# Layer 1 of a hybrid RWKV-7 / attention / Hyena backbone: two scans run as one sequence

## The chip, the cores and the metric

The kernel runs on one core of a Trainium2 chip. That core has five engines with a program of their own each: TensorE (PE, with its weight loads as PEld), VectorE (DVE), ScalarE (ACT), GpSimd (POOL) and SyncE (SP), which issues most DMA transfers. Each engine takes its instructions in the order in which they were written down for it; semaphores order the engines among each other. The metric is the device time of one execution in microseconds, lower is better.

## The reference

Two layers work on 256 context tokens and 512 latent tokens of width 1024. Each layer normalises its tokens, projects them once, and hands the columns to three mixers (RWKV-7 in both directions, latent attention, Hyena convolution); a joint output projection and an expert network (PEER) follow. In the last layer only the latents go on, but the RWKV state that the latents start from and the attention keys and values of the context are still needed. Cut to the part that the change touches:

```python
def rwkv7_mixer(p_lat, p_ctx, ..., need_ctx):
    lr, lk, lv, ldec, la, lkk, lkr, lg = rwkv7_prepare(p_lat, *prm)
    cr, ck, cv, cdec, ca, ckk, ckr, cg = rwkv7_prepare(p_ctx, *prm)
    for d, rev in enumerate((False, True)):
        s_ctx, yc = rwkv7_scan(s0, cr, cdec[d], ckk, ca[d], ckr[d], cv, rev)
        _, yl = rwkv7_scan(s_ctx, lr, ldec[d], lkk, la[d], lkr[d], lv, rev)
    ...
    S = S * w_t - (S kk_t) (kk_t * a_t) + v_t k_t     # one step of a scan
    y_t = S r_t
# layer 1 (need_ctx is False): the context scan gives s_ctx and no y
    out = concat([rwkv, attention, hyena]) @ w_out    # waits for all three
```

## The kernel before

The six RWKV heads are three pairs (`j` = 0, 1, 2), one pair on 128 partitions. A scan is done in chunks of 64 tokens, both directions at once. A step of `rwkv` is one pair and one group of 256 tokens per direction (`s`): the context has one group a pair, the latents two, so layer 1 has three context steps and six latent steps. A step has two parts.

- `prep` (`rwkv_keys` for the first group of a pair, then `rwkv_group`) needs the projected columns but no state: decays by a scan along the tokens (`L`, `Pt`), the products `EH` and `FG`, and then the inverse of a triangular matrix by five levels of small products (`Ahz`, `X`, `Dz`, `Xz`), which go to and fro between PE, DVE and ACT. It ends with `Ktok` and `Btok`.
- `chain` (`rwkv_chain`) carries the state `S` through the four chunks of the group: `R`, `U`, then `S` (DVE, line 1052 is the last row of a chunk), for the latents also the output `Y`. After the second group of a latent pair, `rwkv_read` normalises `Y` and turns it back by 24 products on PE (lines 777 and 272, `rw<-ident,Y`, `rw<-eye,Y`).

In one call of `rwkv`, `merge` writes the `chain` of a step and the `prep` of the next one interleaved, so that the `prep` fills the waits of the `chain`. Layer 1 calls `rwkv` twice, first for the context and then for the latents. Between the calls it closes the pools of the context (`zc`, `rwk`, `rwp`) and opens `rwk` and `rwp` anew, at twice the width. The last `chain` of the context and the first `prep` of the latents therefore stand in different calls.

`layer1` weaves four tracks: `context_out`, `attention` (which projects latents and context, then runs `mla` for the context and for the latents), `scan`, and `hyenas`. `weave` always takes the track whose summed cost is lowest; the costs are the numbers that the generators yield, those of the scan times `RC1` = 0.05 for the context and `RL1` = 0.8 for the latents. What is woven is then put into its final order on each engine by the scheduler of the tile framework, which follows priority and readiness as it models them.

`mla` for the latents works on three groups of two heads. For a group it makes keys (`kTl`) and queries (`qT`) from `x`; then, for each head, eight products for the row maxima (`mm<-kTc,qT`, `mm<-kTl,qT`, reduced by DVE to `mx`, `top`), and six rounds of score product (`tr<-qT,...`), exponential on ACT (`PT`, line 1225) and product with the values (`mm<-PT,...`). The score tile `tr` has one buffer in PSUM, so that a round's score waits for the exponential of the round before. A reciprocal and a multiplication on DVE (lines 1231 and 1233) end a head. When scan, attention and Hyena are written, `mixed` begins the output projection (`mhi`, `mlo`, `mm<-mlo,wh`); it needs the heads of all three.

Of the kernel before, what the change touches and what calls it, by code (L numbers as in the profile page):

```python
# [10 lines left out]
F32 = mybir.dt.float32  # L11
# [11 lines left out]
TC, TL = 256, 512  # L23
# [127 lines left out]
RC1, RL1 = 0.05, 0.8  # L151
# [93 lines left out]
class K:  # L245
# [294 lines left out]
    def layer1(self):  # L540
        if self.done:
            return
        with ExitStack() as lay, ExitStack() as es:
            zl = self.open_layer(1, lay, 2)
            zkv = self.lp.tile([128, 2, TC], F32, name="zkv")
            yml = [zl[:, 11], zl[:, 15], zl[:, 12]]
            ctx = ExitStack()
            z = {}

            def scan():  # L550
                yield self.after("rwc")
                yield from self.scaled(self.rwkv(1, (0, z["c"], False)), RC1)
                ctx.close()
                self.rwk = [es.enter_context(self.pool(n, k)) for n, k in (("rwk", 1), ("rwp", 2))]
                self.mark("rw1")
                yield from self.scaled(self.rwkv(1, (1, zl, True)), RL1)

            def hyenas():
                yield from self.hyena_filters(1, 1, "left")
                self.mark("flt")  # L560
                yield self.after("rw1")
                yield from self.hyena(1, 1, zl, "left")

            def attention():
                self.wcut = 4
                yield from self.project(1, 1, [(m, zl[:, m]) for m in ORDER], "right", self.h1)
                self.wcut = 8
                self.scale_par()
                self.mark("pl1")
                yield self.after("xc1", "flt")  # L570
                self.open_rwkv(es)
                zc = z["c"] = ctx.enter_context(self.pool("zc")).tile([128, 7, TC], F32, name="zc")
                self.rwk = [ctx.enter_context(self.pool(n, k)) for n, k in (("rwk", 1), ("rwp", 2))]
                self.mark("rwc")
                yield from self.project(1, 0, [(m, zc[:, m - 3] if m < 10 else zkv[:, m - 19]) for m in ORDER if m in (3, 4, 5, 6, 7, 8, 9, 19, 20)], "right")
                yield from self.mla(1, 0, [None, None, zkv[:, 0], zkv[:, 1]], None, "right")
                yield from self.mla(1, 1, [zl[:, m] for m in range(17, 21)], yml, "right")

            self.weave((0, self.context_out()), (0, attention()), (0, scan()), (0, self.scaled(hyenas(), HL1)))
            es.close()  # L580
            self.open_late(1)
            self.flat(self.mixed(1, 1, [zl[:, 0], zl[:, 1], zl[:, 2], *yml, zl[:, 13], zl[:, 14]], "left"))
        if self.done:
            return
        self.flat(self.ffn(1))
        self.late.close()
        self.dump("xf11", [self.x[1][:, k] for k in range(8)])
# [188 lines left out]
        else:  # L776
            self.nc.tensor.transpose(out, src, self.ident[h, h])

    def rwkv(self, li, *jobs):

        nc = self.nc
        if self.done:
            return
        H = (slice(0, 64), slice(64, 128))
        wd, ws = self.rwd, self.rws
        wk, wp = self.rwk
        if True:
            W = max(TL if b else TC for b, _, _ in jobs)
            alloc = lambda n, T, **k: wk.tile([128, W], F32, name=n, **k)[:, :T]
            keys, vy, made = {}, {}, {}  # L790

            def parts(b, z, full, j):
                T = TL if b else TC
                o = 0 if full else -3
                return T, z[:, 9 + o], z[:, j] if full else None, z[:, 3 + o + j], z[:, 6 + o + j]

            def prep(b, z, full, j, s, ready):
                T, zd, zr, zk, zv = parts(b, z, full, j)
                nseg = T // 256
                if s == 0:  # L800
                    if j == 0:
                        yield self.after(*[("z", li, b, m) for m in ((9, 10) if full else (9,))])
                        nc.scalar.activation(zd[0:64], zd[0:64], AF.Tanh)
                        if full:
                            nc.scalar.activation(z[:, 10], z[:, 10], AF.Tanh, scale=0.5)
                            nc.vector.tensor_scalar(z[:, 10], z[:, 10], 0.5, 0.5, op0=OP.mult, op1=OP.add)
                    yield self.after(*[("z", li, b, m) for m in ((j, 3 + j, 6 + j) if full else (3 + j, 6 + j))])
                    keys[b, j] = self.rwkv_keys(j, T, zk, alloc)
                sg2 = (s, nseg - 1 - s)
                tok = [slice(256 * g, 256 * g + 256) for g in sg2]  # L810

                def dv(ap):
                    v = ap.rearrange("p (g t) -> p g t", t=256)
                    if nseg == 1:
                        return v[:, 0:1, :].to_broadcast([128, 2, 256])
                    return v if s == 0 else v[:, ::-1]

                made[b, j, s] = yield from self.rwkv_group(j, tok, dv, zd, zr, zk, *keys[b, j], full, wp, wd, ws, H, ready)

            def chain(b, z, full, j, s):  # L820
                T, zd, zr, zk, zv = parts(b, z, full, j)
                nseg, nch = T // 256, T // 64
                c3 = lambda ap: ap.rearrange("p (c t) -> p c t", t=64)
                if s == 0:
                    Vt = c3(alloc("Vt", T))
                    self.to_tok(Vt, [zv[:, 64 * c:64 * c + 64] for c in range(nch)])
                    vy[b, j] = Vt, c3(alloc("Y", T)) if full else None
                Vt, Y = vy[b, j]
                yield from self.rwkv_chain(j, s, (s, nseg - 1 - s), *made[b, j, s], Vt, Y, nch, full, ws, H)
                if s == nseg - 1:  # L830
                    if full:
                        self.rwkv_read(j, T, Y, zr, zk, Vt, z[:, 10], zr, alloc)
                        yield 5
                    if j == 2:
                        self.mark(("rwkv", li, b))

            steps = [(b, z, full, j, s) for b, z, full in jobs for j in range(3) for s in range((TL if b else TC) // 256)]
            yield from prep(*steps[0], self.after())
            for n, g in enumerate(steps):
                def scan(g=g, n=n):  # L840
                    yield from chain(*g)
                    self.mark(("chain", li, g[0], n))
                if n + 1 < len(steps):
                    yield from self.merge(scan(), prep(*steps[n + 1], self.after(("chain", li, g[0], n))))
                else:
                    yield from scan()

    def merge(self, *gens):

# [953 lines left out]
```

## Time and profile before

| What | Value |
|---|---|
| median of 3 runs | 5459.62 us (5457.41 to 5464.74) |
| profiled execution, own time | 5464.84 us |
| its span, first to last instruction | 5463.1 us |
| mean granted TensorE clock | 0.928 |
| busy share of PE, PEld, DVE, ACT, POOL | 90%, 69%, 70%, 35%, 23% |

The span is the time from the first to the last instruction of the profiled execution, and that execution took 1.7 us more than its span and 5.2 us more than the median. All times in the rows below are microseconds from the start of the span. The mixers of layer 1, where the change lies, stand between about 3380 and 4061 us.

### The profile page before, as it was taken

What the parts mean: (1) busy time and instruction counts of PE and PEld (TensorE: products, weight loads), DVE (VectorE), ACT (ScalarE), POOL (GpSimd) and SP (SyncE); (2) the same over time, 40 slices, a digit from 0 to 9 for tenths busy, and PEclk for the clock granted to TensorE, in tenths of its full rate; (3) what the DMA queues carried; (4) which work ended last, traced back from release to release, by engine and by line L of the source; (5) the groups of instructions that cost most, each with busy time, mean ns of one, the idle gap of its engine ahead of it and who ended that gap; (6) DMA issues with size and microseconds to landing.
All of it is one profiled execution on the core that took longest, in us unless ns stands there. A gap on an engine that the chain in (4) does not pass through costs nothing. (4 is left out here: it accounts for less than half of the span.)

```text
span 5463.1 us, 76042 instructions
## 1 busy us (share of the span) xinstructions
PE 4928.4 (90%) x28693; PEld 3745.5 (69%) x28693; DVE 3849.6 (70%) x8277; ACT 1918.5 (35%) x3438; POOL 1241.3 (23%) x933
## 2 busy tenths in 40 slices
PE   7987998889989999999999678888889889999998
PEld 4765676547644588887878456656657667888887
DVE  6356666656896488887888875656646985777776
ACT  5322222443254333333333232222223454444442
POOL 2322212221200122222222363211122321111110
PEclk9977899899999999999999889777899999999999
DMA  6300121342365788888888764200022668888885
GB/s 207 103 22 31 51 86 55 113 151 71 109 187 162 240 326 316 330 323 311 318 325 303 274 238 153 77 1 1 1 74 82 196 191 295 324 322 312 321 320 206
DMA packets 395517, 1028.18 MB, mean 188 GB/s; under 512 B 31780, under 2 KB 198981, under 8 KB 339597
## 3 DMA queue, kind: packets, MB, share of 16 engines
q1 hardware_dynamic: 339852, 620.65, 34.0%
q0 software_dynamic: 55296, 402.68, 19.6%
q8 instruction: 225, 3.69, 0.3%
q14 instruction: 144, 1.17, 0.1%
HBM read 920.19 MB, written 103.02 MB: 187 GB/s over the span
## 5 line engine op out<-in xcount | busy, mean ns | idle before, releaser
L203 POOL DMA_INDIRECT row<-in_uv,idx x384 | 531.8, 1385 | 1860.8 <-DVE acc L241 1586.7
L659 ACT ACTIVATE wh<-w 128x1024 fp32r<-128x1024 f32 (+1 forms) x557 | 571.0, 1027 | 1049.5 <-PE mm L272 461.7
L272 PE MATMUL mm<-hlo,wh 128*128 128x512 f32 (+2 forms) x2408 | 877.0, 368 | 30.7 <-DVE zl L688 7.5
L272 PE MATMUL mm<-hhi,wh 128*128 128x512 f32 (+2 forms) x2408 | 866.8, 364 | 0.0
L660 DVE TENSOR_TENSOR wl<-w,wh 128x1024 fp32r<-128x1024 f32 x424 | 516.3, 1221 | 255.0 <-ACT wh L659 252.1
L272 PE MATMUL mm<-hhi,wl 128*128 128x512 f32 (+2 forms) x2408 | 531.5, 361 | 1.7 <-POOL wl L660 1.7
L272 PEld LDWEIGHTS mm<-hlo,wh 128*128 128x128 f32 x2408 | 461.2, 192 | 104.4 <-issue 18.4
L241 DVE SCALAR_TENSOR_TENSOR acc<-row,act,acc 128x1024 f32<-128x1024 f32 x381 | 496.5, 1303 | 35.3 <-ACT act L237 34.6
L272 PEld LDWEIGHTS mm<-hhi,wh 128*128 128x128 f32 x2408 | 461.5, 192 | 61.8 <-issue 3.3
L219 DVE SCALAR_TENSOR_TENSOR row<-row,xk 128x1024 f32<-128x1024 f32 x384 | 480.3, 1251 | 16.5 <-DMA row<-in_uv,idx 16.3
L272 PE MATMUL mm<-row,wh 128*128 128x512 f32 (+1 forms) x1056 | 455.5, 574 | 29.9 <-DMA wh<-in_uT 25.1
L272 PEld LDWEIGHTS mm<-hhi,wl 128*128 128x128 f32 x2408 | 425.9, 189 | 56.6 <-issue 3.8
L660 POOL TENSOR_TENSOR wl<-w,wh 128x1024 fp32r<-128x1024 f32 (+1 forms) x133 | 291.4, 2198 | 670.0 <-ACT wh L659 405.3
L272 PEld LDWEIGHTS mm<-row,wh 128*128 128x128 f32 x1056 | 195.3, 195 | 211.2 <-issue 165.4
L236 ACT ACTIVATE act<-act 128x1 f32<-128x1 f32 x384 | 75.7, 197 | 498.6 <-DVE row L219 498.3
L1779 ACT ACTIVATE stage<-ch 128x512 f32<-128x512 f32 x224 | 218.2, 1101 | 62.6 <-PE ch L272 59.8
L1546 ACT ACTIVATE g<-mm 128x512 f32<-128x512 f32 (+1 forms) x256 | 137.6, 538 | 232.3 <-PE mm L272 197.2
L272 PE MATMUL rw<-wh,cl 128*128 128x512 f32 x512 | 201.5, 394 | 6.5 <-DVE cl L1614 3.5
L272 PE MATMUL rw<-wl,ch 128*128 128x512 f32 x512 | 200.5, 392 | 0.0
L272 PE MATMUL rw<-wh,ch 128*128 128x512 f32 x512 | 199.9, 390 | 0.0
L272 PE MATMUL ch<-wh,cl 128*128 128x512 f32 x512 | 199.6, 390 | 0.0
L272 PE MATMUL ch<-wh,ch 128*128 128x512 f32 x512 | 199.4, 389 | 0.0
(542 smaller groups left out, 10206.0 us busy)
## 6 DMA issues: line engine op xcount, KB each, us to landing
w<-in_uv SPq DMA_DIRECT2D x256, 512.0 KB
w<-in_uT SPq DMA_DIRECT2D x190, 512.0 KB
Wd<-stage SPq DMA_DIRECT2D x28, 2048.0 KB
w<-in_mod_w SPq DMA_DIRECT2D x192, 256.0 KB
wh<-in_uT SPq DMA_DIRECT2D x66, 512.0 KB
W<-Wd SPq DMA_DIRECT2D x32, 1024.0 KB
W<-Wd SPq DMA_DIRECT2D x32, 768.0 KB
w<-in_wq SPq DMA_DIRECT2D x32, 512.0 KB
```

The costliest lines, as they stand in the source:

```text
L203: self.nc.gpsimd.indirect_dma_start(out=row, out_offset=None, in_=self.k.io[f"uv{self.li}"], in_offset=bass.IndirectOffsetOnAxis(ap=self.t ...
L219: nc.vector.scalar_tensor_tensor(row[:, 0:1024], row[:, 0:1024], 1.0, self.x, op0=OP.mult, op1=OP.mult, accum_out=act)
L236: nc.scalar.activation(act, act, AF.Gelu)
L241: nc.vector.scalar_tensor_tensor(self.acc, row[:, 1024:], act, self.acc, op0=OP.mult, op1=OP.add)
L272: self.nc.tensor.matmul(out, lhsT, rhs, start=start, stop=stop, skip_group_check=True)
L659: self.nc.scalar.activation(wh[:, s], w, AF.Copy)
L660: eng.tensor_tensor(wl[:, s], w, wh[:, s].bitcast(F32), op=OP.subtract)
L1546: nc.scalar.activation(g, p[:, 0:ND], AF.Gelu)
L1779: nc.scalar.activation(stage[:, :, u:u + 4].rearrange("p a t -> p t a"), p, AF.Copy, scale=1 / GS)
```

## The change

Layer 1 now calls `rwkv` once with both jobs, so that `merge` also joins the last `chain` of the context with the first `prep` of the latents. The pools `rwk` and `rwp` are opened once, and `zc` stays open with them. The cost factor moves into `rwkv`: a merged step is scaled by the factor of the step whose `chain` it holds, so the first latent `prep` is now woven at `RC1` and no longer at `RL1`. The Hyena track waits for the mark that ends the context scan instead of the mark `rw1`.

```diff
-            ctx = ExitStack()
             z = {}
 
             def scan():
                 yield self.after("rwc")
-                yield from self.scaled(self.rwkv(1, (0, z["c"], False)), RC1)
-                ctx.close()
-                self.rwk = [es.enter_context(self.pool(n, k)) for n, k in (("rwk", 1), ("rwp", 2))]
-                self.mark("rw1")
-                yield from self.scaled(self.rwkv(1, (1, zl, True)), RL1)
+                yield from self.rwkv(1, (0, z["c"], False), (1, zl, True), cost=(RC1, RL1))
 
             def hyenas():
                 yield from self.hyena_filters(1, 1, "left")
                 self.mark("flt")
-                yield self.after("rw1")
+                yield self.after(("rwkv", 1, 0))
                 yield from self.hyena(1, 1, zl, "left")
...
-                zc = z["c"] = ctx.enter_context(self.pool("zc")).tile([128, 7, TC], F32, name="zc")
-                self.rwk = [ctx.enter_context(self.pool(n, k)) for n, k in (("rwk", 1), ("rwp", 2))]
+                zc = z["c"] = es.enter_context(self.pool("zc")).tile([128, 7, TC], F32, name="zc")
+                self.rwk = [es.enter_context(self.pool(n, k)) for n, k in (("rwk", 1), ("rwp", 2))]
...
-    def rwkv(self, li, *jobs):
+    def rwkv(self, li, *jobs, cost=(1.0, 1.0)):
...
-            yield from prep(*steps[0], self.after())
+            yield from self.scaled(prep(*steps[0], self.after()), cost[steps[0][0]])
             for n, g in enumerate(steps):
                 def scan(g=g, n=n):
                     yield from chain(*g)
                     self.mark(("chain", li, g[0], n))
-                if n + 1 < len(steps):
-                    yield from self.merge(scan(), prep(*steps[n + 1], self.after(("chain", li, g[0], n))))
-                else:
-                    yield from scan()
+                tracks = [scan()] + [prep(*x, self.after(("chain", li, g[0], n))) for x in steps[n + 1:n + 2]]
+                yield from self.scaled(self.merge(*tracks), cost[g[0]])
```

No instruction of the scan, of the attention or of Hyena is added or dropped; their order on the engines changes. Two places matter.

The first place is ACT, where the context scan ends and the latents begin. `Ktok`, `Btok` and `Vt` belong to the scan, `kka<-zl` is the first row of the first latent `prep` and `sg`, `ta`, `Pt`, `L` are its next ones; `sx`, `x`, `kTl`, `Vl` are the attention of the latents and `pr` is Hyena. Before, the last `chain` of the context runs while the attention's first rows pass (`Vl`, and `x` and `sx` for the keys), of which the two on top are the last, and `kka<-zl` stands behind them:

```order
L1167 ACTIVATE x<-mm,rmy 128x2x64
L1175 ACTIVATE sx<-x 128x192
L878 ACTIVATE kka<-zl,rvec 128x512
L1200 ACTIVATE kTl<-tr,qkc 96x512 x2
L1164 ACTIVATE x<-mm,rmy 128x192 x2
L1175 ACTIVATE sx<-x 128x192 x2
L1164 ACTIVATE x<-mm,rmy 128x192
L1175 ACTIVATE sx<-x 128x192
L906 ACTIVATE sg<-rw,hvec_27250 128x256 x2
L922 ACTIVATE ta<-rw,hvec_27250 128x256 x2
```

In the changed kernel, whose line numbers are lower by five to seven, `kka<-zl` stands seventeen rows ahead of the first row shown here, and the `prep` follows the context's last `Vt` at once:

```order
L999 ACTIVATE Ktok<-rw 128x512
L999 ACTIVATE Btok<-rw 128x512
L1055 ACTIVATE Vt<-rw 128x256
L899 ACTIVATE sg<-rw,hvec_27250 128x256 x2
L915 ACTIVATE ta<-rw,hvec_27250 128x256 x2
L1384 ACTIVATE pr<-hy 128x256
L907 ACTIVATE Pt<-L 128x512
L909 ACTIVATE L<-L 128x512
```

So the `prep` has moved up past the start of the latents' attention (`Vl`, `x`, `sx`, `kTl`), and that attention has moved down behind it; the keys `kTl` of the first two heads now stand behind the `prep`'s `Btok`.

The second place is ACT at the end of the stage, from the last row of the last `chain` on. `qT<-tr 1x512` begins the rounds of a head, each `PT` is one round, `sq<-Y` belongs to the last `rwkv_read`, and `mhi`, `wh` to the output projection. Before:

```order
L1218 ACTIVATE qT<-tr 1x512
L1225 ACTIVATE PT<-tr 128x512 x3
L748 ACTIVATE mhi<-zl 128x512 x2
L1225 ACTIVATE PT<-tr 128x512
L748 ACTIVATE mhi<-zl 128x512
L1076 ACTIVATE sq<-Y 128x512
L748 ACTIVATE mhi<-zl 128x512 x2
L1225 ACTIVATE PT<-tr 128x512
L748 ACTIVATE mhi<-zl 128x512
L1225 ACTIVATE PT<-tr 128x512
L1218 ACTIVATE qT<-tr 1x512
L748 ACTIVATE mhi<-zl 128x512
```

And in the changed kernel:

```order
L1069 ACTIVATE sq<-Y 128x512
L743 ACTIVATE mhi<-zl 128x512 x2
L1193 ACTIVATE qT<-tr,qkc 96x512 x2
L743 ACTIVATE mhi<-zl 128x512
L654 ACTIVATE wh<-w 128x1024
L1211 ACTIVATE qT<-tr 1x512
L654 ACTIVATE wh<-w 128x1024
L1218 ACTIVATE PT<-tr 128x512 x6
L1211 ACTIVATE qT<-tr 1x512
L1218 ACTIVATE PT<-tr 128x512 x6
L743 ACTIVATE mhi<-zl 128x512
```

Before, the queries of the last two heads, the maxima of the last but one and four of its six rounds stood ahead of `sq<-Y`; now the queries of the last two heads, all sixteen maxima products and all twelve rounds stand behind it. PE's order shows the same: its last rows of the last `chain` are followed by eight transposes of `x` for these queries.

## Rows read from the trace of the kernel before

**Rows 1.** Windows: stretch, length, busy PE, PEld, DVE, ACT, POOL; clock, DMA share, GB/s.
```profile
3563.40:3582.30 18.90, 17.21 (x192) 12.26 (x192) 9.62 (x51) 5.05 (x13) 2.62 (x3) 0.85 0.01 2
3582.30:3644.20 61.90, 45.35 (x329) 32.82 (x329) 39.84 (x114) 17.79 (x36) 8.67 (x7) 0.72 0.00 1
3644.20:4009.20 365.00, 313.18 (x3242) 222.64 (x3243) 227.89 (x614) 96.39 (x192) 45.30 (x36) 0.81 0.01 1
4009.20:4061.10 51.90, 37.23 (x92) 15.68 (x90) 20.74 (x38) 12.23 (x20) 8.46 (x5) 0.77 0.12 40
```

**Rows 2.** Timeline of ACT: start, length, line, operation, [idle before, releaser].
```profile
3563.43 0.38 ACT L1062 ACTIVATE Vt<-rw 128x256 f32<-128x256 f32 x1 [1.97 <-PE rw L272]
...
3581.97 0.72 ACT L878 ACTIVATE kka<-zl,rvec 128x512 f32<-128x512 f32 x1 [5.31 <-PE ch L272]
...
3593.36 0.84 ACT L906 ACTIVATE sg<-rw,hvec 128x256 f32<-128x256 f32 x2 [2.04 <-PE rw L272]
...
3637.91 0.60 ACT L1006 ACTIVATE Ktok<-rw 128x512 f32<-128x512 f32 x1 [3.26 <-PE rw L272]
...
3644.20 0.60 ACT L1062 ACTIVATE Vt<-rw 128x512 f32<-128x512 f32 x1 [3.90 <-PE rw L272]
```

**Rows 3.** Timeline of ACT: first and last rows of two later `prep` parts without `rwkv_read`.
```profile
3646.20 0.84 ACT L906 ACTIVATE sg<-rw,hvec 128x256 f32<-128x256 f32 x2 [1.40 <-PE rw L272]
...
3699.55 0.60 ACT L1006 ACTIVATE Ktok<-rw 128x512 f32<-128x512 f32 x1 [5.85 <-PE rw L272]
...
3942.39 0.84 ACT L906 ACTIVATE sg<-rw,hvec 128x256 f32<-128x256 f32 x2 [1.40 <-PE rw L272]
...
3987.73 0.60 ACT L1006 ACTIVATE Ktok<-rw 128x512 f32<-128x512 f32 x1 [5.72 <-PE rw L272]
```

**Rows 4.** Timeline of DVE: ends of chunks of the scan, last reciprocal and multiplication.
```profile
3571.51 0.28 DVE L1052 TENSOR_TENSOR S<-S,Pc 128x128 f32<-128x128 f32 x1
...
4008.99 0.28 DVE L1052 TENSOR_TENSOR S<-S,Pc 128x128 f32<-128x128 f32 x1
...
4018.00 3.36 DVE L1231 RECIPROCAL rc<-mm 64x512 f32<-64x512 f32 x1 [0.26 <-PE mm L272]
...
4025.49 0.16 DVE L1214 TENSOR_REDUCE top<-mx 128x4 f32<-128x8 f32 x1
...
4060.40 0.69 DVE L1233 TENSOR_TENSOR zl<-mm,rc 64x512 f32<-64x512 f32 x1
```

**Rows 5.** Timeline of PE: maxima products, last `rwkv_read`, first score of the last head.
```profile
4010.46 0.60 PE L272 MATMUL mm<-kTc,qT 96*128 96x256 f32 x2
...
4013.19 1.02 PE L272 MATMUL mm<-kTl,qT 96*128 96x512 f32 x2
...
4028.11 0.31 PE L777 MATMUL rw<-ident,Y 64*64 64x64 f32 x1 [3.38 <-POOL Y L1093]
...
4033.23 1.87 PE L272 MATMUL tr<-ident,top 128*1 128x128 f32 x8
...
4035.78 2.08 PE L272 MATMUL tr<-qT,kTl 97*128 97x512 f32 x2 [0.68 <-ACT qT L1218]
```

**Rows 6.** Timelines of ACT and POOL: query of the last group; rounds of the last heads.
```profile
3970.09 1.47 POOL L1194 TENSOR_TENSOR x<-x,rq0y 128x768 f32<-128x768 f32 x1 [9.22 <-DVE x L1193]
3973.64 0.68 ACT L1200 ACTIVATE qT<-tr,qkc 96x512 f32<-96x512 f32 x1 [1.90 <-PE tr L1198]
...
4013.45 0.60 ACT L1225 ACTIVATE PT<-tr 128x512 f32<-128x512 f32 x1
...
4016.18 0.60 ACT L1225 ACTIVATE PT<-tr 128x512 f32<-128x512 f32 x1 [1.62 <-PE tr L272]
...
4037.89 0.60 ACT L1225 ACTIVATE PT<-tr 128x512 f32<-128x512 f32 x1 [1.51 <-PE tr L272]
4042.42 0.60 ACT L1225 ACTIVATE PT<-tr 128x512 f32<-128x512 f32 x1 [3.93 <-PE tr L272]
```

**Rows 7.** Windows: a stretch inside the last head, columns as in the first group.
```profile
4025.00:4045.00 20.00, 14.78 (x41) 6.69 (x42) 2.00 (x4) 4.30 (x6) 3.86 (x4) 0.50 0.15 52
```

## What the change does to the time: the prediction

> **What bounds this part now.** I first cut the mixers of layer 1 into stretches by the windows view, then followed the scan in the timeline of ACT, whose rows mark the steps of `prep`, and last I read the end of the stage on PE, ACT and DVE. The windows [rows 1] show four stretches. In 3563 to 3582 us the last `chain` of the context runs without a `prep`: 18.9 us, PE busy for 17.2 of them, since Hyena and the attention of the latents run beside it. In 3582 to 3644 the first latent `prep` runs without a `chain`: 61.9 us with PE busy for 45.4, so PE idles 16.5. In 3644 to 4009 `chain` and `prep` run merged, with attention as filler: 365 us, PE busy 313.2 (86%). From 4009 to 4061 the scan is over and the attention of the last two heads ends the stage: 51.9 us, PE busy 37.2, idle 14.7. So PE is nearly full except where a serial chain of small operations has nothing beside it, and the stage ends with the attention, not with the scan: the last multiplication of the last head starts at 4060.40, 51.4 us after the last row of the scan's last chunk at 4008.99 [rows 4]. Whoever speeds up the scan must ask where the attention goes.
>
> **The change part by part.** *The serial piece that is removed.* `kka`, the first row of the first latent `prep`, stands idle until 3581.97, released by a `ch` product of the context's last `chain` [rows 2]; in the order before it is behind that `chain`. In the new order it stands ahead, and only the first of the four chunks is still in front of the decays. That chunk ends at 3571.51 + 0.28 [rows 4]; from a `Vt` to the next `sg` a merged step takes 3644.20 to 3646.20, 2.0 us [rows 2, 3]. So `sg` should come at 3573.8 and not at 3593.36 [rows 2]: **19.6 us earlier**.
>
> *What the merge costs the `prep`.* Alone it takes from `sg` to `Ktok` 3593.36 to 3637.91, 44.6 us [rows 2]. Beside a `chain` and without a readout the shortest takes 45.3 (3942.39 to 3987.73) and the longest 53.4 (3646.20 to 3699.55) [rows 3]. I take the middle, 49.4: **4.8 us back**, between 0.7 and 8.8. The first step thus gains 14.8, between 10.8 and 18.9, the upper end being the whole length of the lone `chain`.
>
> *Work that leaves the six merged steps.* The attention now starts behind this `prep`, about a head later relative to the scan. What stood ahead of 4009 and goes behind it are some ten maxima products, five of 0.60 and five of 1.02 us [rows 5], and three rounds of two products of that larger shape, 2.04 each: 8.1 + 6.1 = 14.2 us of PE. Were the merged steps bound by PE alone, 86% of that would be gained, 12.2; were they bound by the scan's own chain, nothing. Within a step PE waits for DVE and ACT at each of five levels, so I take a value nearer to zero: **5 us**, between 0 and 12.2. The last chunk of the scan then ends 19.8 us earlier, at about 3989, between 10.8 and 31.1 earlier.
>
> *What that work costs at the end.* Behind the last chunk now stand, by the new order: the rest of the queries of the last group. On POOL and PE this takes 3970.09 to 3973.64, 3.6 us, and POOL had waited 9.2 for DVE [rows 6]; part of that will have passed, so I take 4.5 of those 9.2, together 8.1. Then eight maxima products, 4 x (0.60 + 1.02) = 6.5, with the readout's turning back of `Y` in their middle, 4028.11 to 4033.23, 5.1 [rows 5]. PE must wait for that `Y`: it came 19.1 us after the last chunk, 3.4 of them behind a reciprocal that now stands elsewhere [rows 4, 5], so 15.8, while PE gets there after 8.1 + 0.7 + 3.2 = 12.0; wait 3.8. From the last product of the readout to the first score 4033.23 to 4035.78, 2.6 [rows 5]. Six rounds at 2.73 (4013.45 to 4016.18) [rows 6], 16.4; the maxima of the last head that lie between cost nothing, as they did at 4010 to 4018. Then reciprocal and remaining maxima, 4018.00 to 4025.65, 7.7 [rows 4]. Last the last head from 4033.23 to the end at 4061.09, 27.9. Sum 8.1 + 6.5 + 5.1 + 3.8 + 2.6 + 16.4 + 7.7 + 27.9 = 78.1 against 51.9 now: **26.2 us more**. With the queries finished and `Y` in time (8.3 less), and the last head's first three rounds at 2.73 and not 4.53 (4037.89 to 4042.42 [rows 6]; 5.4 less), it is 12.5 more; with queries and clock against it, 42.8 more.
>
> *Edits that I cost at nothing.* The pools: `rwk` is as wide for the context as for the latents, but the operations keep their lengths; one reopening goes, and its price is the wait of `kka`, already counted. Hyena's start at another mark: its rows keep their places up to the context's last `chain`, and its last product only has to be ready for the output projection, hundreds of microseconds later. DMA: SP's order is the same.
>
> *The clock.* In 4025 to 4045, inside the last head, PE's granted clock is 0.50 [rows 7], that is 1.2 GHz, after a stretch in which PE waited for DVE's reciprocal and for `Y`; rounds there take 4.53 and not 2.73. In the new order the wait for the queries comes right behind the scan, so the maxima and the first rounds may fall under the same half clock: twice the time, so 6.5 more, for the maxima and 3 x 1.8 for three rounds. The Trainium skill, "TensorE: Matmul & The Clock Gate", Part 1, says that the throttled state is the default and that activity releases it; the trace agrees here with its 0.50 behind that wait. I leave this out of the sum, since in the new order maxima products fill the rounds, and make it a rival.
>
> **Sum.** Scan 19.8 earlier, end 26.2 longer: 6.4 us slower. The profiled execution would take 5464.84 + 6.4; the median of the three runs lies 5.2 below it, so 5459.6 + 6.4 = **5466.0 us**. A measurement of this kernel can tell about 0.2%, 11 us, from no change, so this counts as no change.
>
> **The rivals.** *Faster: the idle time of PE is simply filled.* The two stretches that the change joins hold 62.6 us of PE work and 16.5 + 1.7 of idle. If that idle is used and PE's idle in the end part stays at 14.7, the stage shortens by the larger part, 16.5: 5443.1 us. For it speaks that the work is the same and PE the fullest engine; against it, that the end part becomes half as long again and consists of rounds that wait for one another. It decides for this rival if PE's idle behind the last chunk grows by less than 5.5 us. The Trainium skill, "Perfetto Trace Analysis", section "Optimization Strategy", says that a kernel whose bound changes over time may gain by interleaving its regimes. By that rule the change gains; here it also takes the interleaving away at the end, where two heads now stand alone.
>
> *Slower: the end runs at half clock.* Place: maxima and rounds of the last but one head. Price: 6.5 + 5.4 = 11.9 on top, so 18.3 slower, 5477.9 us. For it speaks the 0.50 above, and that PE has only eight transposes between the scan and the queries; against it, that the maxima come without gaps and may bring the clock back soon. It decides from about 5 us of added cost on, for then the sum passes 11.
>
> *The merge does not reach the first latent `prep`,* because something else holds `kka`. In the order nothing of that kind stands ahead, and the same join works in all later steps; time 5459.6. I give it little and count it with no change.
>
> **How the numbers follow.** No change within 0.2%: 0.42, my own sum and the last rival. Slower by more: 0.34, the half clock, a late query, or a `prep` that suffers more from the `chain`. Faster by more: 0.24, the filled idle, helped by the 12.2 of the third term. The ends of the terms taken all one way give 18.6 faster and 32.0 slower; all at once is unlikely, so the range is 5443 to 5488 us; the likeliest case's own is 5453 to 5472.
>
> **What would show it.** Right: `sg` of the first latent `prep` near 3574, its `Ktok` near 3623, the last `S` row of the scan near 3989, and some 78 us from there to the last head's multiplication, at about 4067. Wrong: a last `S` row later than 4000 (the `prep` then lost what the join gave), or less than 65 or more than 90 us behind it; a clock of 0.50 over the rounds of the last but one head would be the half-clock rival. The rest of the program, before 3380 and behind the output projection, should keep its length; a difference there would be none of my terms.

## The result: half a per cent slower

| | before | after |
|---|---|---|
| median of 8 runs, us | 5458.77 (5452.23 to 5472.04) | 5481.45 (5467.15 to 5515.23) |
| span of the profiled execution, us | 5463.1 | 5480.7 |
| mean granted clock over the span | 0.928 | 0.924 |

The ratio of after to before is 1.0051, 95% interval 1.0031 to 1.0071. The time lies inside the range of the forecast, and slower is the way that its sum pointed (6.4 us), but the change is clearly slower, and not "no change", the likeliest case; the rival with the half clock (5477.9) is nearest.

To see where the 17.6 us of the spans came from, I cut both traces at the same three rows: the context's last `Vt`, the `Ktok` of the first latent `prep`, and the scan's last `S`. The windows view of before, its first two stretches (columns as in [rows 1]; the third, behind the scan, is 52.1 us long):

```profile
3563.40:3637.90 74.50, 56.26 (x482) 40.42 (x483) 49.45 (x164) 21.64 (x45) 11.29 (x9) 0.75 0.00 1
3637.90:4009.30 371.40, 319.57 (x3282) 227.39 (x3282) 227.99 (x614) 97.59 (x194) 45.30 (x36) 0.81 0.01 1
```

The same view of after, all three stretches:

```profile
3550.90:3611.40 60.50, 47.21 (x458) 38.90 (x459) 39.98 (x122) 17.04 (x36) 7.91 (x6) 0.69 0.00 1
3611.40:3988.10 376.70, 326.65 (x3286) 233.22 (x3285) 230.65 (x652) 101.26 (x202) 47.69 (x38) 0.80 0.01 1
3987.80:4071.50 83.70, 61.43 (x138) 26.57 (x138) 29.34 (x61) 16.20 (x26) 10.33 (x6) 0.70 0.07 25
```

The joined step is 14.0 us shorter, the six merged steps are 5.3 longer, and the end is 31.6 longer. What stands ahead of the context's last `Vt`, from the first `kka` of the context on, took 191.1 and 186.8, 4.3 less. Together 18.6 us, which accounts for the 17.6 us of these two spans, since the rest of the program takes 4774.3 and 4773.4. That the rest comes out alike is luck: over all traces of this document it lies between 4771 and 4806 us, so the stage is what traces are compared by, and the ratio of all timed runs says what the program gains or loses. The bracket behind PE's busy time counts its instructions (an fp32 product is mostly two). The joined step lost 24 of them, the stretch ahead of it 28 (1465 and 1437), the end gained 46 (92 before), and the six merged steps have 4 more.

The timeline of ACT in after, which answers to [rows 2]: the join works.

```profile
3550.92 0.38 ACT L1055 ACTIVATE Vt<-rw 128x256 f32<-128x256 f32 x1 [1.97 <-PE rw L272]
...
3561.18 0.84 ACT L899 ACTIVATE sg<-rw,hvec 128x256 f32<-128x256 f32 x2 [9.87 <-PE rw L272]
...
3611.40 0.60 ACT L999 ACTIVATE Ktok<-rw 128x512 f32<-128x512 f32 x1 [3.01 <-PE rw L272]
```

From `Vt` to `sg` are 10.3 us in place of 29.9 [rows 2]. The end of the stage, in rows of DVE, POOL and PE of after that answer to [rows 4, 5]:

```profile
3987.80 0.28 DVE L1045 TENSOR_TENSOR S<-S,Pc 128x128 f32<-128x128 f32 x1
...
3992.42 1.86 POOL L1187 TENSOR_TENSOR x<-x,rq0y 128x768 f32<-128x768 f32 x1 [6.93 <-DVE vr L1072]
...
3994.33 1.09 PE L1191 MATMUL tr<-ident,x 128*96 128x128 f32 x4 [6.88 <-DVE rgy L284]
...
3997.93 1.91 PE L272 MATMUL mm<-kTl,qT 96*128 96x512 f32 x2
...
4003.01 0.31 PE L772 MATMUL rw<-ident,Y 64*64 64x64 f32 x1 [0.30 <-POOL Y L1086]
...
4011.84 2.08 PE L272 MATMUL mm<-kTl,qT 96*128 96x512 f32 x2
...
4017.54 2.08 PE L272 MATMUL tr<-qT,kTl 97*128 97x512 f32 x2 [0.68 <-ACT qT L1211]
...
4037.00 3.36 DVE L1224 RECIPROCAL rc<-mm 64x512 f32<-64x512 f32 x1 [1.01 <-PE mm L272]
...
4044.40 1.87 PE L272 MATMUL tr<-ident,top 128*1 128x128 f32 x8 [0.98 <-DVE top L1207]
...
4070.77 0.69 DVE L1226 TENSOR_TENSOR zl<-mm,rc 64x512 f32<-64x512 f32 x1
```

PE stands idle for 6.88 us right behind the scan, since POOL gets the queries only when DVE has dealt with the readout's sums, whose rows stand among DVE's last ones for these queries. Then the maxima of 512 columns take 1.91 and 2.08 us each where they took 1.02 [rows 5]. The windows of after over the same stretch show why (the last three numbers are clock, DMA share, GB/s):

```profile
3987.00:3992.00 5.00, 0.46 (x13) 0.32 (x9) 5.00 (x24) 3.75 (x7) 0.00 (x0) 0.91 0.00 0
3992.00:4003.00 11.00, 7.60 (x16) 3.64 (x16) 8.41 (x24) 1.36 (x2) 5.64 (x4) 0.50 0.00 0
4003.00:4024.00 21.00, 18.55 (x47) 8.61 (x48) 4.12 (x8) 3.93 (x5) 4.68 (x2) 0.50 0.30 101
4024.00:4041.00 17.00, 13.19 (x31) 5.32 (x29) 6.63 (x8) 2.98 (x5) 0.00 (x0) 0.96 0.00 0
4041.00:4055.00 14.00, 11.52 (x23) 4.78 (x24) 1.95 (x5) 1.78 (x3) 0.00 (x0) 0.55 0.00 0
```

PE falls to half clock (1.2 GHz) behind the idle time at the scan's end, and again behind the wait for the reciprocal at 4037.

### The profile page after: what moved, and what is told of

Its sections match the earlier page's. It is cut to its first block, busy times and chain, and to the rows that moved or that the text cites. A ratio compares the mean times of both kernels' runs of the same rounds, so it can differ in the third digit from the quotient of the medians.

```text
span 5480.7 us, 76059 instructions
## 1 busy us (share of the span) xinstructions
PE 4944.4 (90%) x28693; PEld 3757.2 (69%) x28693; DVE 3848.1 (70%) x8277; ACT 1918.0 (35%) x3438; POOL 1237.5 (23%) x933
## 3 DMA queue, kind: packets, MB, share of 16 engines
q0 software_dynamic: 55296, 402.68, 19.5%
## 5 line engine op out<-in xcount | busy, mean ns | idle before, releaser
L272 PE MATMUL mm<-hlo,wh 128*128 128x512 f32 (+2 forms) x2408 | 880.8, 370 | 32.7 <-ACT wh L654 11.9
```

Of the source, the lines that this page charges most:

```text
L272: self.nc.tensor.matmul(out, lhsT, rhs, start=start, stop=stop, skip_group_check=True)
```

## The experiments

**The theory.** The joined step gains what was forecast, but the stretch that it closes had been where the latents' attention found room. That attention now runs a head behind the scan, and at the end two heads stand alone, in rounds that wait for one another, at half clock. **Rivals:** the pools and not the join do it; the clock alone makes the end long; or the stage costs the sum of PE's work wherever the attention stands.

All twelve runs in one table. "Scan" is from the first context `kka` to the last `S`, "end" from there to the end of the last head's multiplication (below zero where that stands ahead of the last `S`), "stage" from the first to the later of the ends of that multiplication and of the last row of the readout, all read from timelines of ACT and DVE, one trace a row. The ratios come from all timed runs.

| kernel | scan | end | stage | ratio to before (95%) |
|---|---|---|---|---|
| before / second trace | 636.7 / 633.6 | 52.1 / 52.1 | 688.8 / 685.7 | 1.0006 (0.9990 to 1.0021), the second |
| after / second trace | 623.7 / 627.2 | 83.7 / 83.7 | 707.3 / 710.9 | 1.0033 (1.0016 to 1.0049), the second |
| pools alone | 619.8 | 83.6 | 703.4 | 1.0064 (1.0043 to 1.0084) |
| clock fill | 617.0 | 80.7 | 697.7 | 1.0030 (1.0015 to 1.0046) |
| join, price 1.5 | 677.4 | -5.4 | 697.1 | 1.0019 (1.0001 to 1.0036) |
| before, price 1.2 | 651.0 | 20.0 | 670.9 | 0.9979 (0.9960 to 0.9998) |
| join, Hyena 1 pair earlier | 618.5 | 52.7 | 671.2 | 0.9979 (0.9966 to 0.9993) |
| join, Hyena 2 pairs earlier | 645.8 | 42.5 | 688.3 | 1.0003 (0.9987 to 1.0019) |
| before, Hyena 1 pair earlier | 633.3 | 41.0 | 674.2 | 0.9966 (0.9950 to 0.9983) |
| before, Hyena 2 pairs earlier | 664.2 | 7.8 | 688.1 | 1.0031 (1.0016 to 1.0047) |
| join, Hyena 1 earlier, price 1.5 | 643.6 | -5.4 | 663.3 | 0.9988 (0.9972 to 1.0004) |
| join, Hyena 1 earlier, two score tiles | 615.3 | 44.8 | 660.0 | 0.9958 (0.9937 to 0.9979) |

**Pools alone.** The calls are one and the pools stay open, but the first latent `prep` is written behind the context's last pair:

```diff
-                tracks = [scan()] + [prep(*x, self.after(("chain", li, g[0], n))) for x in steps[n + 1:n + 2]]
+                nxt = steps[n + 1:n + 2]
+                seam = nxt and nxt[0][0] != g[0]
+                tracks = [scan()] + [prep(*x, self.after(("chain", li, g[0], n))) for x in nxt if not seam]
                 yield from self.scaled(self.merge(*tracks), cost[g[0]])
+                if seam:
+                    yield from self.scaled(prep(*nxt[0], self.after()), cost[1])
```

> One call and pools that stay open, but no join: the first latent preparation is written behind the context's last pair, and priced as the latents are. Theory (the reopened pools were what held the first latent preparation behind the chain; once they stay open the order on the engines overlaps the two without the join, and the attention falls a head behind the scan): as the changed kernel, ratio to the kernel before 1.003 to 1.007, about 83 us from the last row of the scan to the last head's product. Rival 1 (the join in the writing does it): as before, ratio 0.998 to 1.002, about 52 us behind the scan.

It behaves as the changed kernel. Its timeline of ACT and its window behind the scan:

```profile
3572.38 0.38 ACT L1059 ACTIVATE Vt<-rw 128x256 f32<-128x256 f32 x1 [1.12 <-PE rw L272]
...
3581.39 0.84 ACT L903 ACTIVATE sg<-rw,hvec 128x256 f32<-128x256 f32 x2 [8.63 <-PE rw L272]
```

```profile
4011.30:4094.90 83.60, 61.39 (x138) 26.46 (x138) 29.32 (x61) 16.20 (x26) 10.32 (x6) 0.70 0.07 25
```

`sg` comes 9.0 us behind `Vt`, as with the join (10.3 and 9.9 in the two traces of after, 8.6 in clock fill, which has the same order up to there), and the same 138 instructions of PE are left at the end. So the join in the writing is not needed. Nor does the price of that step matter: priced as context in the kernel before, or as latents in the changed one, it leaves each kernel's order on PE, ACT, DVE and POOL row for row as it was. The new mark for Hyena, put alone into the kernel before, leaves its order as it was too, and that kernel with its two calls, but with pools that stay open (opened at the latents' width), has the latents' attention behind the scan as the changed kernel has it. These four were not run. What is left of the diff is the lines that no longer close and reopen the pools: with these open, the scheduler under the kernel puts this `prep` beside the `chain` by itself.

**Second traces** of both kernels:

> The changed kernel once more, for a second trace of it. Theory (the join gains what the forecast gave the scan, and the first profile was a slow one of it): from the first context key row to the scan's last row 615 to 622 us in place of 623.7, end part 83 to 84; stage 698 to 706; ratio 1.003 to 1.007. Rival (the scan of the changed kernel really gains only 13): 622 to 626.

> The kernel before once more, for a second trace of it: how far two traces of one kernel lie apart in this stage. If the stage repeats: scan 633 to 640 us, end part 51 to 53, stage 685 to 692. If the 4 to 7 us by which the scans of kernels with the same order differed are chance of single executions, it may lie as far away: scan 628 to 643. Ratio 0.998 to 1.002 in both.

The ends repeat to 0.1 us, the scans within 3.5. The two stretches ahead of the end in the second traces, of before:

```profile
3570.00:3642.40 72.40, 55.07 (x482) 40.24 (x483) 49.05 (x164) 21.63 (x46) 11.29 (x9) 0.74 0.00 1
3642.40:4018.80 376.40, 324.44 (x3282) 230.88 (x3282) 227.60 (x614) 97.48 (x194) 45.29 (x36) 0.80 0.00 1
```

and of after:

```profile
3549.80:3609.70 59.90, 46.65 (x460) 38.62 (x459) 40.09 (x123) 17.09 (x37) 7.92 (x6) 0.69 0.01 1
3609.70:3989.60 379.90, 331.07 (x3286) 234.89 (x3284) 230.82 (x652) 101.21 (x202) 47.68 (x38) 0.79 0.00 1
```

The joined step is 12.5 us shorter here, the six merged steps 3.5 longer, the stage 25.2 longer, though the spans of these two executions differ by 6.2 only: the rest took 4790.0 and 4771.0. The six merged steps by themselves differ by 5.0 us between the two traces of before and by 3.2 between those of after. What I had expected for the scan, that its first profile understated the gain, fell: 627.2 against 623.7.

**Clock fill.** Spare products keep PE busy in the gap behind the scan:

```diff
                 if s == nseg - 1:
+                    if li and full and j == 2:
+                        p = self.ps("hy")
+                        for _ in range(6):
+                            self.mm(p[0:64], self.S[:, 0, j], zr)
                     if full:
```

Their result is not read; the kernel computes what it did. On PE the edit also puts three more of the maxima products ahead of the turning back of `Y`.

> The changed kernel with six spare products of 64x512 on the scan's last state, whose result nobody reads, in the gap of 6.9 us in which PE waits for the last queries. Theory of the half clock (this gap drops the granted clock to 0.50 for the maxima and the first round behind it): maxima at 0.60 and 1.02 us in place of 1.06 and 2.0, 6.5 us less, and one round of 4.5 at 2.7; the end part 72 to 78 us in place of 83, ratio to before 1.001 to 1.004. Rival (the length of the end part comes from the serial rounds and the clock costs little, or the gap is not what lowers it): 81 to 85 us, ratio 1.004 to 1.007.

Rows of PE and two windows of this kernel:

```profile
3987.57 5.36 PE L272 MATMUL hy<-zl,S 128*64 128x512 f32 x12 [0.69 <-DVE S L1049]
...
3996.10 1.02 PE L272 MATMUL mm<-kTl,qT 96*128 96x512 f32 x2
...
4003.34 0.24 PE L772 MATMUL rw<-ident,Y 64*64 64x64 f32 x1 [1.76 <-POOL Y L1090]
```

```profile
3987.00:4003.00 16.00, 11.67 (x34) 4.66 (x34) 14.17 (x45) 5.12 (x9) 5.36 (x4) 1.00 0.00 1
4003.00:4021.00 18.00, 14.75 (x42) 6.76 (x42) 2.05 (x4) 3.91 (x6) 3.34 (x3) 0.53 0.16 59
```

The maxima run at full clock, 1.02 in place of 1.91, and PE then waits 1.76 us for the readout's `Y`, which comes 16.1 us behind the last `S` (15.2 in after). Seven of the eight maxima products are done by then, four in after, and the end falls by 3.0 us, not by 5 to 11: the first half of the maxima had lain inside the wait for `Y`, and the clock falls again behind that wait. Of the 9.6 us of stage against after only these 3.0 belong to the edit; ahead of the last `S` the two kernels have the same order on PE, and the rest is the scatter of single traces. Its ratio, 1.0030, can't be told from the 1.0033 of after's second runs. The clock in this gap alone is not the cause; a kernel whose whole end runs at full clock was not made.

**The attention's place, by price.** A dearer scan of the latents lets the attention go ahead. In the changed kernel (and with 1.2 in the kernel before):

```diff
-RC1, RL1 = 0.05, 0.8
+RC1, RL1 = 0.05, 1.5
```

> The changed kernel with the latents' scan priced 1.5 in place of 0.8, so that in the order one product of the attention is left behind the scan in place of two heads. Theory (the join gains some 13 us in the scan and loses them to two heads that stand alone at the end): the scan's last row comes later, 4000 to 4025 us in place of 3988, since 16 maxima products and 12 rounds, some 37 us of PE, go into the last merged steps; behind it stands the readout alone, 20 to 28 us in place of 83; 22 to 47 us less than the changed kernel, ratio to before 0.994 to 0.999. Rival (the stage is bound by the sum of PE's work, wherever the attention stands): as the changed kernel, ratio 1.003 to 1.007.

> Control: the kernel before (two calls, pools reopened) with the latents' scan priced 1.2, which leaves four rounds of the attention behind the scan in the order. Theory: some 10 maxima products and 6 rounds, about 20 us of PE, go into the merged steps and the end falls from 52 to 25 to 32 us, so 3 to 18 us less than before, ratio 0.9967 to 0.9995; the joined kernel with its higher price is ahead of it by the join's own 10 to 15 us. Rival (the join has no gain of its own): both come out alike, within 5 us.

The first expectation missed by far: the last `S` came 53.7 us later (4062.5 on the trace), not 12 to 37. Up to the last step the kernel runs as the changed one does (its last `sg` is 552.0 us into the stage, 550.0 in after); then what was left of two heads falls into one step. From `sg` to `Ktok` it takes 81.2 us (49.2 in after), as the timeline of ACT shows:

```profile
3937.14 0.84 ACT L899 ACTIVATE sg<-rw,hvec 128x256 f32<-128x256 f32 x2 [1.15 <-PE rw L272]
...
4018.32 0.60 ACT L999 ACTIVATE Ktok<-rw 128x512 f32<-128x512 f32 x1 [2.25 <-PE rw L272]
```

The stage gains 10.2 us on after (13.8 on its second trace) and still loses 8 to 11 on before. In the kernel before, whose last step takes less with its four rounds left behind the scan, the price gains 15 to 18 us of stage, with an end of 20.0 us and not 25 to 32, the first ratio here that beats the kernel before. The joined kernel was not ahead of it, as the control's theory had it, but 26 us behind.

**The attention's place, by Hyena.** The latents' attention waits at the end of each head for Hyena, and Hyena for the whole context. Letting Hyena go one pair earlier (two with a last index of 0; in the kernel before the line replaced has the mark `rw1`) starts the attention earlier:

```diff
-                yield self.after(("rwkv", 1, 0))
+                yield self.after(("chain", 1, 0, 1))
                 yield from self.hyena(1, 1, zl, "left")
```

> The changed kernel with the latents' Hyena let go one pair of context heads earlier, so that the latents' attention, which waits for it, starts earlier too: in the order the same attention is left behind the scan as in the kernel before (6 maxima products, 9 scores, 10 value products), and the join stays. Theory (the change lost in the end part what it gained in the scan): the end part falls from 83.6 back to 50 to 56 us; the head that is taken back costs the scan 0 to 14 us; the stage from the first context key row to the last head 672 to 690 us against 688.8 before and 703 to 707 after; ratio to before 0.996 to 1.001. Rival (PE's work sums up wherever it stands, and the join trades nothing): end part shorter and scan longer by the same, stage 700 to 707, ratio 1.003 to 1.007.

> As the last, with Hyena let go two pairs earlier: one head less, six rounds, left behind the scan. Theory: end part 24 to 32 us, scan 625 to 650, stage 655 to 680 us, 9 to 34 less than before, ratio 0.994 to 0.9985. Rival (PE's work sums up): 700 to 707, ratio 1.003 to 1.007.

> Control without the join: the kernel before with Hyena let go one pair earlier. In the order it leaves behind the scan the same rows as the joined kernel with Hyena two pairs earlier, so these two differ by the join at equal ends. If the join has a gain of its own (the first term of the forecast, 14.8 us of the first latent step), the joined one is 8 to 18 us shorter in the stage. If the join only moves one head of the attention from the seam to the end, and an order with equal ends takes equal time, both are within 5 us. Against the kernel before: end part 24 to 32 us, stage 660 to 680, ratio 0.995 to 0.999.

> Control without the join and with Hyena two pairs earlier: in the order one score and one value product are left behind the scan, so the readout ends the stage. Theory: behind the scan's last row some 20 us of readout; the scan takes the last head's maxima and rounds in its last step, 645 to 665 us; stage 665 to 685, ratio 0.995 to 0.999, no better than with one pair earlier, since the readout now ends it. Rival (each head taken from the end gains again): 640 to 660, ratio 0.990 to 0.994.

The joined kernel with Hyena one pair earlier leaves the same rows behind the scan as the kernel before. The windows of its joined step, its six merged steps and its end:

```profile
3568.70:3620.20 51.50, 37.00 (x440) 30.06 (x440) 41.84 (x153) 16.38 (x34) 10.18 (x8) 0.83 0.01 2
3620.20:4001.50 381.30, 332.03 (x3302) 234.52 (x3302) 230.53 (x619) 99.28 (x196) 45.29 (x36) 0.79 0.01 1
4001.20:4053.80 52.60, 38.40 (x92) 16.66 (x90) 20.87 (x39) 12.23 (x20) 8.46 (x5) 0.71 0.11 40
```

The end is back at 52.6 us with 92 instructions, and the stage is 14.5 to 17.6 us shorter than before. The rival of the sum of PE's work is out: the same 5316 instructions of PE take 671.2 us of stage where after's order takes 707.3 and 710.9. That the gain on before is the join's own is not shown by this pair, since Hyena's place differs too. The second such pair (before with Hyena one earlier, join with two) has equal ends too, 41.0 and 42.5, but longer ones than the 24 to 32 expected, and the joined stage is 14.1 us longer where I expected it shorter: Hyena two pairs earlier slows the context's own pairs, whose second `Vt` comes 143.6 and 143.0 us into the stage in the two kernels that have it, and 120 in before and after. That delay is more than both miss their stages by (688.3 for 655 to 680, 688.1 for 665 to 685). From the context's last `Vt` on the joined one is the shorter by 18.4 us (478.0 and 496.4), but with 26 fewer of PE's instructions, which Hyena's earlier start has moved ahead of it.

The join by itself is seen where Hyena is moved alike. With one pair the kernel before reaches 674.2 and the joined one 671.2, and their ratios overlap. The joined step, the six merged steps and the end of this kernel before:

```profile
3559.60:3633.00 73.40, 59.43 (x478) 41.03 (x479) 48.63 (x161) 19.43 (x39) 10.34 (x8) 0.73 0.01 1
3633.00:4015.30 382.30, 328.50 (x3287) 229.64 (x3287) 234.15 (x618) 98.52 (x194) 44.75 (x36) 0.79 0.00 1
4015.00:4055.90 40.90, 31.33 (x68) 12.23 (x67) 14.80 (x32) 10.66 (x17) 8.51 (x5) 0.61 0.14 50
```

The joined scan is 14.8 shorter and its end 11.7 longer: the join again sends part of the attention to the end. With two pairs the joined scan is 18.4 shorter (645.8 and 664.2), and the stages are alike (688.3 and 688.1); the ratio there, 1.0003 against 1.0031, is better than the stages say, and no run shows why. So the join shortens the scan in all three pairs of kernels with Hyena alike, by 6 to 18 us; that it shortens the whole stage is shown in none.

**Together.** Two last versions of the joined kernel with Hyena one pair earlier:

```diff
-                        p = self.ps("tr")[:, :T]
+                        p = self.ps("hy" if li and b and g3 == 2 and n % 2 else "tr")[:, :T]
```

and, in the other, the price of 1.5 as above.

> Join, Hyena one pair earlier, and the latents' scan priced 1.5: in the order one product of the attention is left behind the scan. Theory: the last head goes into the last merged step, which it lengthens by 15 to 30 us, and the readout alone, some 20, stands behind the scan in place of 52.7: stage 660 to 675 against 671.2 without the price, ratio 0.996 to 0.999. Rival (the last step is overfilled, as it was with the price alone, where it took 81 us in place of 49): 675 to 695, ratio 0.999 to 1.004.

> Join, Hyena one pair earlier, and the scores of the last two heads in two buffers in turn, so that a round need not wait until the score before it has been read. Theory (the end part is set by rounds in series): two rounds in 4.6 to 5.0 us in place of 5.5, so 1.5 to 2.7 less over the last head's six rounds, and what the head before it leaves behind the scan shortens by 1 to 3; end part 46 to 50 in place of 52.7. Rival (the readout, 15 us to Y and 5 of turning back, and the half clock set it): 51 to 54.

The price gains 7.9 us of stage (663.3), but its ratio can't be told from 1, nor from that without the price; this is one trace, and the timed runs do not bear it out. Two score tiles shorten the end by 7.9. The first and last `PT` rows of the last head on ACT, with one tile and then with two:

```profile
4030.07 0.60 ACT L1218 ACTIVATE PT<-tr 128x512 f32<-128x512 f32 x1 [1.51 <-PE tr L272]
...
4047.95 0.60 ACT L1218 ACTIVATE PT<-tr 128x512 f32<-128x512 f32 x1 [2.14 <-PE tr L272]
```

```profile
4021.08 0.60 ACT L1218 ACTIVATE PT<-tr 128x512 f32<-128x512 f32 x1 [2.16 <-PE tr L272]
...
4030.42 0.60 ACT L1218 ACTIVATE PT<-hy 128x512 f32<-128x512 f32 x1 [0.26 <-PE hy L272]
```

The six rounds start 17.9 us apart with one tile and 9.3 with two. I had priced a round at full clock, 2.73, and six at 1.5 to 2.7 us less; under the half clock behind the readout a round in series takes 4.5, and there a second buffer saves most. Part of it is also that products of the output projection, which had slipped into the rounds, now stand behind them. The Trainium skill, "Perfetto Trace Analysis", section "Matmuls", asks independent products to rotate through PSUM banks so that one is emptied while the next runs; the 8.5 us agree, less what the products of the output projection have in them, which no run took apart. This version beats both kernels: 0.9958 (0.9937 to 0.9979). Its interval still overlaps with those of Hyena one pair earlier alone, with the join and without it, and the kernel before with two score tiles was not made.

## Why the prediction was right in its range and wrong in its likeliest case

- *The serial piece that is removed* was right: `sg` was to come 19.6 us earlier, and against `Vt` it did by 19.7 (29.9 to 10.3), in the second traces by 17.3 (27.2 to 9.9). The reason was named only in part: I put the wait of `kka` down to the order, and what released it were the pools, as the order with these alone kept open shows.
- *What the merge costs the prep* was right: 4.8 forecast, `sg` to `Ktok` 44.6 to 50.2, 5.7 measured; the step gained 14.0 and 12.5 in the two pairs of traces (14.8 forecast).
- *Work that leaves the six merged steps* is the step that failed. It said that 14.2 us of PE's work leave these steps and that 5 us are gained, between 0 and 12.2. The work that went to the end is as counted (46 instructions more behind the scan), but it came out of the joined stretch and the one ahead of it, 24 and 28 fewer; the six steps hold 3286 in place of 3282, so nothing left them, and they took 5.3 and 3.5 us more and gained nothing. I had compared what stood ahead of 4009 in the two orders and not asked in which stretch of the scan it had stood. The sum is 10.3 us too fast by it.
- *What that work costs at the end* was right in its mechanism and too small: 31.6 for 26.2. Its parts, forecast and measured: from the last `S` to the turning back of `Y` 15.1 and 15.2, the turning 5.1 and 5.1, the other half of the maxima 3.3 and 5.8, to the first score 2.6 and 3.6, six rounds 16.4 and 19.5, reciprocal and maxima 7.7 and 7.4, last head 27.9 and 27.1. The 5.6 us in the third and fifth of these are the half clock; the 1.0 in the fourth is a wait of PE, 1.07, for DVE's `top`.
- *The clock* as a rival had the right place. Its price of 11.9 was too high: the first half of the maxima lies in the wait for `Y`, which clock fill showed, and one round and a half were slow, not three (the scores of the first four rounds start 4.6, 3.8 and 2.7 us apart). To the page that I had cited for it (the Trainium skill, "TensorE: Matmul & The Clock Gate", Part 1: activity releases the throttle) the trace agrees only in part: 4003 to 4024 stayed at 0.50 with PE busy 18.55 of 21 us.
- *The faster rival* named its own test, PE's idle time behind the last chunk: it grew from 14.7 to 22.3 us, by 7.6, and the rival needed less than 5.5. The rule on interleaving that stood beside it (the Trainium skill, "Perfetto Trace Analysis", "Optimization Strategy") did not hold for this change. With Hyena one pair earlier the joined kernel is 14.5 to 17.6 us of stage ahead of before at an end of equal length, but 11.5 to 14.6 come with Hyena's place in the kernel before as well.
- *Edits that I cost at nothing*: of the pools this was wrong as a matter of cause, since keeping them open does the whole change without the join; in the sum it changed nothing. Hyena's new mark is idle, as I had it. That Hyena's start sets where the attention stands I had not seen: one pair earlier is worth 11 to 15 us of stage in the kernel before and 36 to 40 in the changed one.

In the sum: 6.4 forecast, 0.8 more in the joined step, 10.3 for the failed step and 5.4 for the end, less the 4.3 ahead of the context's last `Vt`, make 18.6; the rest of the program is 0.9 shorter, and the spans differ by 17.6. The 4.3 is not an effect of the change: in the second traces that stretch is 2.6 longer in after (187.7 and 185.1). What stays open is whether the six steps, with four instructions more, take longer at all: 371.4 and 376.4 us in the two traces of before, 376.7 and 379.9 in those of after, 379.7 with the pools alone and 376.7 in clock fill. Their clock is 0.01 lower in each pair, and no run took that apart.

## What to carry to other kernels

Before a serial stretch is closed, count what other work runs in it, by instructions and not by time: here that work went where nothing covers it, behind the scan, and 46 instructions of PE cost 31.6 us. Look at what holds an early start, since under a scheduler that reorders it can be a pool that is closed and reopened, and not the order in which the code is written. And if a filler ends a stage alone, start it earlier or give its rounds a second buffer before anything is taken out of the main chain.

## What the hardware showed that I had not expected

- The stage's loss is nearly all in PE's busy time. The same 5316 instructions from the first context `kka` to the last head took 578.2 us before and 594.3 after, at a mean clock of 0.80 and 0.78, while PE's idle time stayed, 110.6 and 113.1, as the windows of the whole stage show, first before, then after:

```profile
3372.30:4061.10 688.80, 578.23 (x5316) 421.62 (x5316) 424.90 (x1157) 182.28 (x362) 101.33 (x84) 0.80 0.07 25
```

```profile
3364.10:4071.50 707.40, 594.33 (x5316) 430.52 (x5316) 424.16 (x1157) 184.84 (x365) 102.21 (x84) 0.78 0.07 24
```

  The second traces say the same: 575.9 and 599.1 busy, 109.8 and 111.8 idle.
- A high busy share and a high clock do not go together here. In clock fill PE was busy 11.67 of 16 us at 1.00, and right behind it 14.75 of 18 at 0.53; the second stretch begins with the 64x64 products that turn `Y` back, after 1.76 us of waiting.
